# The first stage of a bidirectional encoder layer: from a scheduler's order to one fixed by hand

## The chip, the cores and the metric

The kernel runs on one core of a Trainium2 chip. The metric is device time in microseconds (us) of one execution. The engines named here are PE (TensorE, matrix products), ACT (ScalarE), DVE (VectorE), POOL (GpSimd) and SP (SyncE, which here only issues transfers). Each takes its own instructions strictly in order and waits on semaphores that other engines raise.

## The reference, cut to what matters

One layer runs over 256 tokens of width 2048: a Mamba-2 mixer in both directions, cross-attention into 256 memory tokens, and a gated feed-forward block, each with a norm ahead of it. Only the beginning matters here:

```
u = rmsnorm(h, mix_norm)                    # h = x, 256 x 2048
proj = u @ w_in                             # split into z, xbc (xs, B, C), dt
xbc = silu(dwconv(xbc, conv_w, conv_b))     # centred convolution over positions
dt = softplus(dt_raw + dt_bias)             # 128 columns: 64 heads, two directions
...
y = y_f + y_b + xs * d_skip                 # two chunked scans over (xs, dt, B, C)
y = rmsnorm(y * silu(z), norm_g)
h = h + y @ w_out
```

All inputs are float32, and the result is close to a float32 one.

## The kernel before

Every float32 matrix factor is split in two: `hi`, the value rounded to the type that PE multiplies fast (`F32R`), and `lo`, what is left. A product of two factors is three matmuls: hi x hi, hi x lo and lo x hi (lines 152 to 154 of `gemm_feat`). ACT writes `hi`, and DVE then computes `lo` from the same source and `hi`, so `lo` always comes after `hi`. For a block of weights (128 x 1024, 0.5 MB, `raw`) these are the lines 106 and 107 of `split_plain`; for x they are the lines 101 and 102 of `split_scaled`, one call for each 128 x 256 half of a PSUM bank, with the norm's gain as a scale.

The first stage (lines 242 to 282) works like this. x lies in DRAM with the tokens in rows, so PE turns it (line 260): each quarter of 512 columns takes 8 transposes into two PSUM banks, which ACT and DVE split into the tiles `unit`. DVE also copies each bank to `x_stage` (line 264), and a transfer keeps it in DRAM for the residual sum much later (line 265). ACT squares x and sums each row (line 270) for the norm's factor; the factor is applied after the products, by way of `r_mix`: a sum, a square root (line 220, with a load of the ACT table), some small DVE instructions, two products that spread it over all partitions (line 281) and a copy (line 282). The first products are those of dt: 128 columns, 16 steps of the contraction, 48 matmuls. Then follow the 512 columns of the first block of x (`project(0)`): eight blocks of weights, 24 matmuls each, 192 in all. Then come B and C of the same group, and so on through the layer. PSUM has two tiles for such products (`ps_g`); dt takes one, the first block of x the other, and the one of B and C has to wait until DVE has read dt's bank, which needs `r_mix` (line 297).

No order is written out: a scheduler with a simulated timeline places every instruction on each engine's queue, and so mixes transposes, splits, squares, copies and products. Pools limit how far loads run ahead: five blocks of raw weights, four of split ones.

## Time and profile before

| | before |
|---|---|
| device time, median of 3 runs | 1862.79 us (1862.3 to 1864.23) |
| the profiled execution | 1863.24 us, span 1861.5 us from the first to the last instruction |
| PE busy | 1842.3 us, 99% of the span |
| DVE busy | 1264.2 us, 68% |
| ACT busy | 1018.2 us, 55% |
| DMA | 358.94 MB, mean 193 GB/s |
| granted clock of TensorE, mean | 0.998 |

The span is the profiled execution from its first instruction to its last; the remaining 1.74 us lie around it. Busy time of PE counts a matmul from its start to its modelled end, and matmuls overlap, so a full PE is not one at its peak. The granted clock is a share of 2.4 GHz, so 0.5 stands for 1.2 GHz.

### The profile page before, as it was taken

What the parts mean: (1) busy time and instruction counts of PE and PEld (TensorE: products, weight loads), DVE (VectorE), ACT (ScalarE), POOL (GpSimd) and SP (SyncE); (2) the same over time, 40 slices, a digit from 0 to 9 for tenths busy, and PEclk for the clock granted to TensorE, in tenths of its full rate; (3) what the DMA queues carried; (4) which work ended last, traced back from release to release, by engine and by line L of the source; (5) the groups of instructions that cost most, each with busy time, mean ns of one, the idle gap of its engine ahead of it and who ended that gap; (6) DMA issues with size and microseconds to landing.
All of it is one profiled execution on the core that took longest, in us unless ns stands there. A gap on an engine that the chain in (4) does not pass through costs nothing.

```text
span 1861.5 us, 29854 instructions
## 1 busy us (share of the span) xinstructions
PE 1842.3 (99%) x11821; PEld 1663.5 (89%) x11821; DVE 1264.2 (68%) x1792; ACT 1018.2 (55%) x1454; POOL 2.3 (0%) x11
## 2 busy tenths in 40 slices
PE   8999999999999999999999999999999999999997
PEld 8999999999999988888888888888888888888886
DVE  6878888988887756655555667666664456666654
ACT  6667667766775645444444455555553345555443
POOL 0000000000000000000000000000000000000000
PEclk9999999999999999999999999999999999999999
DMA  8667666766766765655655556566666666666563
GB/s 289 198 203 214 199 189 201 219 197 201 215 182 205 244 197 182 184 177 170 176 176 181 164 187 206 179 189 188 191 191 192 193 192 188 185 187 187 190 193 114
DMA packets 289708, 358.94 MB, mean 193 GB/s; under 512 B 11616, under 2 KB 210656, under 8 KB 289056
## 3 DMA queue, kind: packets, MB, share of 16 engines
q1 hardware_dynamic: 289488, 356.76, 62.3%
q8 instruction: 92, 1.51, 0.3%
q14 instruction: 48, 0.39, 0.1%
q0 software_dynamic: 80, 0.28, 0.1%
HBM read 352.60 MB, written 4.39 MB: 192 GB/s over the span
## 4 chain that ended last, share of the span: by engine, by line
PE 99%; DMA 0%; DVE 0%; ACT 0%; SPq 0%; issue 0%; DVEq 0%
PE psg L169 30%; PE psg L171 16%; PE psg L154 10%; PE psg L153 10%; PE psg L152 10%; PE psm L194 6%; PE psm L193 6%; PE psm L195 6%; PE psm L453 1%; PE psm L448 1%; PE psm L419 1%; PE psm L589 0%; PE psm L591 0%; PE psm L590 0%; DMA x<-in_x_dram 0%; PE psm L405 0%
## 5 line engine op out<-in xcount | busy, mean ns | idle before, releaser
L107 DVE TENSOR_TENSOR w_lo<-raw,w_hi 128x1024 fp32r<-128x1024 f32 x618 | 753.7, 1223 | 499.3 <-ACT w_hi L106 497.1
L106 ACT CAST w_hi<-raw 128x1024 fp32r<-128x1024 f32 x618 | 645.7, 1049 | 684.0 <-PE psg L169 314.5
L169 PE MATMUL psg<-unit,w_hi 128*128 128x512 f32 x2432 | 853.3, 396 | 0.0
L171 PE MATMUL psg<-unit,w_lo 128*128 128x256 f32 x2432 | 683.4, 281 | 0.0
L169 PEld LDWEIGHTS psg<-unit,w_hi 128*128 128x128 f32 x2432 | 456.3, 188 | 106.0
L171 PEld LDWEIGHTS psg<-unit,w_lo 128*128 128x128 f32 x2432 | 460.7, 189 | 0.2
L154 PE MATMUL psg<-unit,w_lo 128*128 128x256 f32 x1552 | 444.8, 287 | 0.1
L152 PE MATMUL psg<-unit,w_hi 128*128 128x256 f32 x1552 | 442.4, 285 | 0.0
L153 PE MATMUL psg<-unit,w_hi 128*128 128x256 f32 x1552 | 441.6, 285 | 0.0
L154 PEld LDWEIGHTS psg<-unit,w_lo 128*128 128x128 f32 x1552 | 298.6, 192 | 3.4 <-issue 3.1
L152 PEld LDWEIGHTS psg<-unit,w_hi 128*128 128x128 f32 x1552 | 298.7, 193 | 1.7 <-issue 1.7
L153 PEld LDWEIGHTS psg<-unit,w_hi 128*128 128x128 f32 x1552 | 298.7, 193 | 0.3 <-issue 0.2
L195 PE MATMUL psm<-w_hi,unit 128*128 128x512 f32 x480 | 187.0, 390 | 0.0
L194 PE MATMUL psm<-w_lo,unit 128*128 128x512 f32 x480 | 187.0, 390 | 0.0
L193 PE MATMUL psm<-w_hi,unit 128*128 128x512 f32 x480 | 186.9, 389 | 0.0
L193 PEld LDWEIGHTS psm<-w_hi,unit 128*128 128x128 f32 x480 | 90.1, 188 | 18.9
L195 PEld LDWEIGHTS psm<-w_hi,unit 128*128 128x128 f32 x480 | 90.1, 188 | 18.8
L194 PEld LDWEIGHTS psm<-w_lo,unit 128*128 128x128 f32 x480 | 90.1, 188 | 18.4
L435 ACT ACTIVATE r<-r,ncum_tok 128x128 f32<-128x128 f32 x128 | 39.4, 390 | 57.5 <-DMA r<-cum_d 57.5
L436 DVE SCALAR_TENSOR_TENSOR r<-r,ncum_tok 128x128 f32<-128x128 f32 x128 | 37.0, 347 | 16.7 <-ACT r L435 16.7
L441 ACT ACTIVATE t<-cb,dt_tok 128x128 f32<-128x128 f32 x128 | 39.1, 389 | 0.7 <-DVE cb L428 0.2
L442 DVE SCALAR_TENSOR_TENSOR t<-cb,dt_tok,t 128x128 f32<-128x128 f32 x128 | 36.5, 349 | 3.3 <-ACT t L441 3.3
(222 smaller groups left out, 1076.4 us busy)
## 6 DMA issues: line engine op xcount, KB each, us to landing
raw<-in_w_up_dram SPq DMA_DIRECT2D x176, 512.0 KB, 3.7
raw<-in_w_in_dram SPq DMA_DIRECT2D x130, 512.0 KB, 4.6
raw<-in_w_down_dram SPq DMA_DIRECT2D x88, 512.0 KB, 3.8
raw<-in_w_out_dram SPq DMA_DIRECT2D x64, 512.0 KB, 4.2
raw<-in_wkv_dram SPq DMA_DIRECT2D x64, 512.0 KB, 3.8
raw<-in_w_in_dram SPq DMA_DIRECT2D x64, 256.0 KB, 4.4
r<-cum_d SPq DMA_DIRECT2D x16, 1024.0 KB, 6.3
raw<-in_wq_dram SPq DMA_DIRECT2D x32, 512.0 KB, 3.5
```

The source lines that it names most:

```text
L106: nc.scalar.copy(out=hi, in_=src)
L107: nc.vector.tensor_tensor(out=lo, in0=src, in1=hi.bitcast(F32), op=ALU.subtract)
L152: nc.tensor.matmul(dst, wh, uh, start=first, stop=False, skip_group_check=True)
L153: nc.tensor.matmul(dst, wh, ul, start=False, stop=False, skip_group_check=True)
L154: nc.tensor.matmul(dst, wl, uh, start=False, stop=last, skip_group_check=True)
L169: nc.tensor.matmul(ps[:, ft, :], hi[:, kk, fs], unit[2][:, kt % 4].rearrange("p s t -> p (s t)"), start=(kt == 0), stop=False, skip_group_ ...
L171: nc.tensor.matmul(ps[:, ft, :T], lo[:, kk, fs], unit[0][:, kt % 4, :], start=False, stop=(kt == nk - 1), skip_group_check=True)
L193: nc.tensor.matmul(banks[tt], uh, hi[:, kk, :], start=(kt == 0), stop=False)
L194: nc.tensor.matmul(banks[tt], uh, lo[:, kk, :], start=False, stop=False)
L195: nc.tensor.matmul(banks[tt], ul, hi[:, kk, :], start=False, stop=(kt == nk - 1))
L435: nc.scalar.activation(out=t1[:, h, :], in_=t1[:, h, :], func=AF.Identity, bias=ncum_tok[:, c, hf:hf + 1])
L441: nc.scalar.activation(out=t2[:, h, :], in_=cb[:, 1, :], func=AF.Copy, scale=dt_tok[:, c, hb:hb + 1])
```

## The change

The first stage is written out in order. `tc.manual_schedule` fixes the order on PE, ACT, DVE and SP for the instructions between its two calls, and the scheduler places only what follows. The steps are small functions: `load_x`, `load_dt`, `load_xw` issue transfers; `busy(n)` issues n products of a tile of ones with itself into an unused bank; `transpose_x`, `split_x`, `keep_x` and `square_x` treat one quarter of x; `split_w` splits a block of weights; `dt_part` and `x_part` issue products. Both PSUM tiles are taken at the start, and the products of the first block of x move from `project(0)` into this stage. The computed values are the same. Ten products of ones are new; no other instruction is added or left out.

```diff
+    def split_raw(raw):
+        hi = sb(ring, [P, raw.shape[1], raw.shape[2]], "w_hi", F32R)
+        lo = sb(ring, [P, raw.shape[1], raw.shape[2]], "w_lo", F32R)
         split_plain(hi, lo, raw)
         return hi, lo
 
+    def load_weights(wv, k0, cols):
+        return split_raw(load_raw(wv, k0, cols))
...
     units_mix = [new_unit() for _ in range(4)]
+    ps_dt, ps_x = psum_g(), psum_g()
     with tc.tile_pool(name="xin", bufs=1) as xin:
+        ordered = tc.manual_schedule(engines={mybir.EngineType.PE, mybir.EngineType.Activation,
+                                              mybir.EngineType.DVE, mybir.EngineType.SP})
+        ordered.__enter__()
         xt = [sb(xin, [P, D], f"x{tt}") for tt in range(2)]
-        dt_w = []
-        for q4 in range(4):
-            if q4 == 2:
-                dt_w.append(load_raw(w_in_v, 0, [(10240, P)]))
+        ss = sb(xin, [P, 2, 4], "x_ss")
+        raws = {}
+        def load_x(u):
             for tt in range(2):
-                nc.sync.dma_start(out=xt[tt][:, q4 * 512:(q4 + 1) * 512],
-                                    in_=x[tt * P:(tt + 1) * P, q4 * 512:(q4 + 1) * 512])
-        ss = sb(xin, [P, 2, 4], "x_ss")
-        for u in range(4):
-            stage = sb(xin, [P, 4, T], "x_stage", bufs=2)
+                nc.sync.dma_start(out=xt[tt][:, u * 512:(u + 1) * 512], in_=x[tt * P:(tt + 1) * P, u * 512:(u + 1) * 512])
+        def load_dt(i):
+            raws["dt", i] = load_raw(w_in_v, 8 * i, [(10240, P)])
+        def load_xw(i):
+            raws["x", i] = load_raw(w_in_v, 2 * i, [(INNER, 512)])
+        def busy(n):
+            for _ in range(n):
+                nc.tensor.matmul(ps_dt[:, 1, :P], ones, ones, start=True, stop=True, skip_group_check=True)
+        def transpose_x(u):
+            out = []
             for jj in range(2):
                 ps = psum_m()
-                for j in range(2):
-                    kt = u * 4 + jj * 2 + j
-                    for tt in range(2):
+                for tt in range(2):
+                    for j in range(2):
+                        kt = u * 4 + jj * 2 + j
                         nc.tensor.transpose(out=ps[:, j * T + tt * P:j * T + (tt + 1) * P],
                                             in_=xt[tt][:, kt * P:(kt + 1) * P], identity=ident)
+                out.append(ps)
+            return out
+        def split_x(u, banks):
+            for jj, ps in enumerate(banks):
                 for j in range(2):
                     split_scaled(units_mix[u], jj * 2 + j, two(ps)[:, j, :], pcol("g_mix", u * 4 + jj * 2 + j))
+        def keep_x(u, banks):
+            stage = sb(xin, [P, 4, T], "x_stage", bufs=2)
+            for jj, ps in enumerate(banks):
                 nc.vector.tensor_copy(out=stage[:, jj * 2:jj * 2 + 2, :], in_=two(ps))
             nc.sync.dma_start(out=xT_d[:, u * 4:(u + 1) * 4, :], in_=stage)
-        dt_bank = gemm_feat(units_mix, w_in_v, [(10240, P)], first_raw=dt_w[0])[0]
-        for q4 in range(4):
+        def square_x(u):
             for tt in range(2):
                 junk = sb(xin, [P, 512], "x_junk")
-                nc.scalar.activation(out=junk, in_=xt[tt][:, q4 * 512:(q4 + 1) * 512], func=AF.Square,
-                                     accum_out=ss[:, tt, q4:q4 + 1])
+                nc.scalar.activation(out=junk, in_=xt[tt][:, u * 512:(u + 1) * 512], func=AF.Square,
+                                     accum_out=ss[:, tt, u:u + 1])
+        def dt_part(i, k0, k1):
+            hi, lo = raws["dt", i]
+            for kt in range(k0, k1):
+                feat_products([ps_dt[:, 0, :]], units_mix, hi[:, kt - 8 * i:kt - 8 * i + 1, :], lo[:, kt - 8 * i:kt - 8 * i + 1, :], kt, 16)
+        def x_part(i):
+            hi, lo = raws["x", i]
+            feat_products([ps_x[:, 0, :], ps_x[:, 1, :]], units_mix, hi, lo, 2 * i, 16)
+        def split_w(kind, i):
+            raws[kind, i] = split_raw(raws[kind, i])
+        load_x(0)
+        load_dt(0)
+        load_xw(0)
+        load_x(1)
+        load_xw(1)
+        busy(6)
+        t = transpose_x(0)
+        split_x(0, t)
+        busy(4)
+        split_w("dt", 0)
+        keep_x(0, t)
+        load_x(2)
+        load_xw(2)
+        dt_part(0, 0, 4)
+        t = transpose_x(1)
+        split_w("x", 0)
+        x_part(0)
+        split_x(1, t)
+        split_w("x", 1)
+        x_part(1)
+        dt_part(0, 4, 8)
+        keep_x(1, t)
+        load_x(3)
+        load_dt(1)
+        load_xw(3)
+        t = transpose_x(2)
+        split_x(2, t)
+        split_w("x", 2)
+        x_part(2)
+        keep_x(2, t)
+        load_xw(4)
+        split_w("x", 3)
+        t = transpose_x(3)
+        x_part(3)
+        split_x(3, t)
+        load_xw(5)
+        split_w("dt", 1)
+        dt_part(1, 8, 12)
+        split_w("x", 4)
+        x_part(4)
+        keep_x(3, t)
+        load_xw(6)
+        square_x(0)
+        square_x(1)
+        dt_part(1, 12, 16)
+        split_w("x", 5)
+        x_part(5)
+        load_xw(7)
+        square_x(2)
+        square_x(3)
+        split_w("x", 6)
+        x_part(6)
+        split_w("x", 7)
+        x_part(7)
+        ordered.__exit__(None, None, None)
+        dt_bank = ps_dt[:, 0, :]
...
         def project(g):
             xs = sb(ssd, [P, 4, T], "xs", bufs=2)
-            conv_silu(gemm_feat(units_mix, w_in_v, [(INNER + g * 512, 512)]), [g * 4 + j for j in range(4)], xs)
+            banks = [ps_x[:, 0, :], ps_x[:, 1, :]] if g == 0 else gemm_feat(units_mix, w_in_v, [(INNER + g * 512, 512)])
+            conv_silu(banks, [g * 4 + j for j in range(4)], xs)
```

On PE, the third quarter of x (banks psm_158 and psm_168) before: its transposes lie among the first products of dt.

```order
L260 MATMUL psm_158<-ident_77,x0_100 128x128 [waits DMAHW5_49,DVE_49,PE_49]
L260 MATMUL psm_158<-ident_77,x1_101 128x128 [waits DMAHW6_49]
L260 MATMUL psm_158<-ident_77,x0_100 128x128
L260 MATMUL psm_158<-ident_77,x1_101 128x128
L152 MATMUL psg_201<-unit_93,w_hi_202 128x256 [waits Activation_49]
L153 MATMUL psg_201<-unit_93,w_hi_202 128x256
L260 MATMUL psm_168<-ident_77,x0_100 128x128 [waits DVE_49,PE_49]
```

On PE, the third quarter now (banks psm_265 and psm_270; w_hi_283 and w_lo_284 are the third block of weights of x, psg_98 its sums).

```order
L146 MATMUL psg_97<-unit_94,w_lo_146 128x256
L277 MATMUL psm_265<-ident_77,x0_104 128x128 [waits DMAHW0_49,PE_49]
L277 MATMUL psm_265<-ident_77,x0_104 128x128
L277 MATMUL psm_265<-ident_77,x1_105 128x128 [waits DMAHW1_49]
L277 MATMUL psm_265<-ident_77,x1_105 128x128
L277 MATMUL psm_270<-ident_77,x0_104 128x128 [waits PE_49]
L277 MATMUL psm_270<-ident_77,x0_104 128x128
L277 MATMUL psm_270<-ident_77,x1_105 128x128 x2
L144 MATMUL psg_98<-unit_94,w_hi_283 128x256 [waits Activation_49]
L145 MATMUL psg_98<-unit_94,w_hi_283 128x256
L146 MATMUL psg_98<-unit_94,w_lo_284 128x256 [waits DVE_49]
```

The eight transposes now stand together, after the last products that the first half of dt's weights allows, and the next instructions behind them are products with the third block of weights.

On ACT before, the same quarter (psm_158, psm_168): squares of x, splits of other banks and casts of weights stand between the halves of one bank.

```order
L101 ACTIVATE unit_95<-psm_158,par_75 128x256 [waits PE_49]
L270 ACTIVATE x_junk_270,x_ss_112<-x1_101 128x512 [waits DMAHW6_49,Activation_49]
L101 ACTIVATE unit_94<-psm_146,par_75 128x256 [waits DVE_49]
L101 ACTIVATE unit_95<-psm_168,par_75 128x256 [waits PE_49]
L270 ACTIVATE x_junk_272,x_ss_112<-x0_100 128x512 [waits DMAHW7_49,Activation_49]
L106 CAST w_hi_232<-raw_230 128x1024 [waits DMAHW1_49]
L101 ACTIVATE unit_95<-psm_158,par_75 128x256 [waits DVE_49]
L270 ACTIVATE x_junk_274,x_ss_112<-x1_101 128x512 [waits DMAHW0_49,Activation_49]
L106 CAST w_hi_362<-raw_360 128x1024 [waits DMAHW2_49]
L101 ACTIVATE unit_95<-psm_168,par_75 128x256 [waits DVE_49]
```

On ACT now, the same quarter (psm_265, psm_270), from the cast before it to the two behind it.

```order
L106 CAST w_hi_215<-raw_115 128x1024 [waits DMAHW6_49]
L101 ACTIVATE unit_95<-psm_265,par_75 128x256 [waits PE_49]
L101 ACTIVATE unit_95<-psm_265,par_75 128x256 [waits DVE_49]
L101 ACTIVATE unit_95<-psm_270,par_75 128x256 [waits PE_49]
L101 ACTIVATE unit_95<-psm_270,par_75 128x256 [waits DVE_49]
L106 CAST w_hi_283<-raw_155 128x1024 [waits DMAHW2_49]
L106 CAST w_hi_317<-raw_263 128x1024 [waits DMAHW7_49,Activation_49]
```

The four halves of a quarter now follow each other directly, and the cast of the weights stands behind them. The wait on DVE in each second half is for DVE's `lo` of the first half of the same bank.

On SP now, the third and the fourth store of turned x (x_stage) and the loads of weights behind them.

```order
L291 DMA xT_d_90<-x_stage_311 128x1024 [waits DMAHW0_49,DVE_49]
L115 DMA raw_315<-in_w_in_dram 128x2x512 [waits DMAHW1_49,Activation_49]
L115 DMA raw_363<-in_w_in_dram 128x2x512 [waits DMAHW2_49,Activation_49]
L291 DMA xT_d_90<-x_stage_409 128x1024 [waits DMAHW3_49,DVE_49]
L115 DMA raw_413<-in_w_in_dram 128x2x512 [waits DMAHW4_49,Activation_49]
L115 DMA raw_463<-in_w_in_dram 128x2x512 [waits DMAHW7_49,DMAHW5_49,Activation_49]
```

Before, all of x, both blocks for dt and the first three blocks for x were issued ahead of the first store; now two or three loads stand behind each store, and each store waits for two DVE copies.

## Rows read from the trace of the kernel before

**Rows 1.** The page, part 4: shares of the chain that ended last, by engine.

```profile
PE 99%; DMA 0%; DVE 0%; ACT 0%; SPq 0%; issue 0%; DVEq 0%
```

**Rows 2.** Windows: stretch (us), its length, busy us (x instructions) per engine, PEclk, DMA share, GB/s.

```profile
12.00:60.00 48.00, 48.00 (x386) 48.00 (x386) 41.60 (x74) 32.76 (x49) 0.00 (x0) 1.00 0.81 259
60.00:540.00 480.00, 479.90 (x4027) 468.65 (x4026) 397.44 (x725) 327.24 (x559) 0.00 (x0) 1.00 0.68 203
600.00:1800.00 1200.00, 1200.00 (x6688) 1045.18 (x6687) 742.24 (x856) 588.40 (x728) 0.00 (x0) 1.00 0.61 188
```

**Rows 3.** Timeline of PE, first stage: start, us busy, what [idle before <- releaser].

```profile
5.16 1.54 PE L260 MATMUL psm<-ident,x 128*128 128x128 f32 x6 [0.73 <-DMA x<-in_x_dram]
...
11.82 0.56 PE L152 MATMUL psg<-unit,w_hi 128*128 128x256 f32 x1
...
12.40 1.05 PE L260 MATMUL psm<-ident,x 128*128 128x128 f32 x4
13.10 0.56 PE L154 MATMUL psg<-unit,w_lo 128*128 128x256 f32 x1
13.46 0.41 PE L152 MATMUL psg<-unit,w_hi 128*128 128x256 f32 x1
...
16.45 0.40 PE L154 MATMUL psg<-unit,w_lo 128*128 128x256 f32 x1
16.66 0.31 PE L152 MATMUL psg<-unit,w_hi 128*128 128x256 f32 x1
```

**Rows 4.** Timeline of PE around the two products of r_b.

```profile
31.82 0.61 PE L281 MATMUL psm<-ident,r_b 128*128 128x128 f32 x4
32.18 0.36 PE L154 MATMUL psg<-unit,w_lo 128*128 128x256 f32 x1
32.38 0.28 PE L152 MATMUL psg<-unit,w_hi 128*128 128x256 f32 x1
32.50 0.28 PE L153 MATMUL psg<-unit,w_hi 128*128 128x256 f32 x1
```

**Rows 5.** Timeline of ACT in the first stage.

```profile
6.36 0.20 ACT L318 ACTIVATE a_neg<-par 128x1 f32<-128x1 f32 x1 [0.43 <-DMA par<-in_params_dram]
6.47 0.46 ACT L101 ACTIVATE unit<-psm,par 128x256 fp32r<-128x256 f32 x1
...
7.82 0.82 ACT L101 ACTIVATE unit<-psm,par 128x256 fp32r<-128x256 f32 x2
8.53 0.63 ACT L270 ACTIVATE x_junk<-x 128x512 f32<-128x512 f32 x1
...
9.14 0.83 ACT L101 ACTIVATE unit<-psm,par 128x256 fp32r<-128x256 f32 x2
9.92 1.05 ACT L106 CAST w_hi<-raw 128x1024 fp32r<-128x1024 f32 x1
...
18.82 1.28 ACT L220 ACT_TABLE_LOAD   x1
```

**Rows 6.** Timeline of DVE in the first stage.

```profile
6.96 0.48 DVE L102 SCALAR_TENSOR_TENSOR unit<-psm,par,unit 128x256 fp32r<-128x256 f32 x1 [0.21 <-ACT unit L101]
...
21.11 1.28 DVE L264 COPY x_stage<-psm 128x512 f32<-128x512 f32 x2
22.31 1.22 DVE L107 TENSOR_TENSOR w_lo<-raw,w_hi 128x1024 fp32r<-128x1024 f32 x1
...
32.98 0.42 DVE L282 COPY r_mix<-psm 128x256 f32<-128x256 f32 x1
33.43 0.42 DVE L297 TENSOR_TENSOR r<-psg,r_mix 128x256 f32<-128x256 f32 x1
```

**Rows 7.** Transfers into raw in the first 30 us, by tile.

```profile
DMA to landing us min/median/max: 4.4/7.0/8.7
```

**Rows 8.** Windows at the end of the span, columns as in rows 2.

```profile
1850.00:1851.00 1.00, 0.39 (x2) 0.00 (x0) 0.57 (x1) 0.52 (x2) 0.00 (x0) 1.00 0.00 0
...
1853.00:1854.00 1.00, 0.00 (x0) 0.00 (x0) 1.00 (x5) 0.72 (x1) 0.00 (x0) 0.54 0.00 0
```

More of the change, by code (lines that the diff above doesn't have):

```diff
@@ L117, in load_raw @@
         return raw
-    def load_weights(wv, k0, cols, raw=None):
-        width = sum(n for _, n in cols)
-        kc = 1024 // width
-        if raw is None:
-            raw = load_raw(wv, k0, cols)
-        hi = sb(ring, [P, kc, width], "w_hi", F32R)
-        lo = sb(ring, [P, kc, width], "w_lo", F32R)
+    def split_raw(raw):
+        hi = sb(ring, [P, raw.shape[1], raw.shape[2]], "w_hi", F32R)
+        lo = sb(ring, [P, raw.shape[1], raw.shape[2]], "w_lo", F32R)
         split_plain(hi, lo, raw)
@@ L127, in load_weights, with feat_products @@
         return hi, lo
+    def load_weights(wv, k0, cols):
+        return split_raw(load_raw(wv, k0, cols))
     def kview(w):
         return w.rearrange("(kt p) n -> p kt n", p=P)
-    def gemm_feat(units, wv, cols, k_first=0, first_raw=None):
+    def feat_products(banks, units, hi, lo, k0, nk):
+        nft = hi.shape[2] // P
+        for kk in range(min(hi.shape[1], nk - k0)):
+            kt = k0 + kk
+            uh = units[kt // 4][0][:, kt % 4, :]
+            ul = units[kt // 4][1][:, kt % 4, :]
+            for ft in range(nft):
+                dst = banks[ft // 2][:, (ft % 2) * T:(ft % 2 + 1) * T]
+                wh = hi[:, kk, ft * P:(ft + 1) * P]
+                wl = lo[:, kk, ft * P:(ft + 1) * P]
+                first = kt == 0 and ft % 2 == 0
+                last = kt == nk - 1 and (ft % 2 == 1 or ft == nft - 1)
+                nc.tensor.matmul(dst, wh, uh, start=first, stop=False, skip_group_check=True)
+                nc.tensor.matmul(dst, wh, ul, start=False, stop=False, skip_group_check=True)
+                nc.tensor.matmul(dst, wl, uh, start=False, stop=last, skip_group_check=True)
@@ L134, in gemm_feat @@
+    def gemm_feat(units, wv, cols):
         width = sum(n for _, n in cols)
-        nft = width // P
-        kc = 1024 // width
         nk = 4 * len(units)
         ps = psum_g()
-        banks = [ps[:, b, :] for b in range((nft + 1) // 2)]
-        for k0 in range(0, nk, kc):
-            hi, lo = load_weights(wv, k_first + k0, cols, first_raw if k0 == 0 else None)
-            for kk in range(kc):
-                kt = k0 + kk
-                uh = units[kt // 4][0][:, kt % 4, :]
-                ul = units[kt // 4][1][:, kt % 4, :]
-                for ft in range(nft):
-                    dst = banks[ft // 2][:, (ft % 2) * T:(ft % 2 + 1) * T]
-                    wh = hi[:, kk, ft * P:(ft + 1) * P]
-                    wl = lo[:, kk, ft * P:(ft + 1) * P]
-                    first = kt == 0 and ft % 2 == 0
-                    last = kt == nk - 1 and (ft % 2 == 1 or ft == nft - 1)
-                    nc.tensor.matmul(dst, wh, uh, start=first, stop=False, skip_group_check=True)
-                    nc.tensor.matmul(dst, wh, ul, start=False, stop=False, skip_group_check=True)
-                    nc.tensor.matmul(dst, wl, uh, start=False, stop=last, skip_group_check=True)
@@ L155, in gemm_feat @@
+        banks = [ps[:, b, :] for b in range((width // P + 1) // 2)]
+        for k0 in range(0, nk, 1024 // width):
+            hi, lo = load_weights(wv, k0, cols)
+            feat_products(banks, units, hi, lo, k0, nk)
         return banks
```

## The prediction

> **What bounds the kernel now.** I read the chain of waits first: it is PE to 99% [rows 1], so what counts is when PE gets its work, and nothing else. The table by stretches says where it lacks it: from 12 us on PE is full in each stretch, with 0.1 us missing between 60 and 540 us and nothing between 600 and 1800 [rows 2]. So a delay of the first stage is paid in full at the end, and a gain there is kept in full. The timeline of PE then shows the first stage. Before 11.82 us there are only transposes, which wait for x. The first product starts at 11.82 and the third, the first one with a `lo` of weights, at 13.10; behind that no wait is left. From 13.46 to 16.45 a product follows every 0.21 us (14 steps in 2.99 us), which is 1.2 GHz, and 0.12 us from there on, which is 2.4 GHz [rows 3, 4]. Four transposes take 0.70 us at the lower clock (12.40 to 13.10), so I count 0.35 at the higher.
>
> The measure for the new order is the start of the products of B and C, since the work ahead of it on PE is the same in both kernels but for the ten products of ones: 32 transposes, 240 products, two for `r_b`. In the old order 103 products stand between `r_b` and that point, so it lies at 32.18 + 103 x 0.12 = 44.5 us [rows 4].
>
> **The price of one quarter of x.** Now a quarter's four halves stand in a row on ACT and DVE, with the cast of the next weights behind them. A half costs ACT 0.46 and DVE 0.48, and DVE begins 0.03 after ACT ends (6.47 + 0.46 = 6.93, then 6.96) [rows 5, 6]. The second half of a bank waits for DVE's first, so it starts at 0.46 + 0.03 + 0.48 + 0.03 = 1.00; the third, in the other bank, follows it after 0.36 (two in 0.82 us [rows 5]); DVE reaches that one at 1.89, after its own second; the fourth waits for it until 2.40. The cast starts at 2.8 and takes 1.05: `hi` is there at 3.85, and `lo`, 1.22 us later, at 5.1 [rows 5, 6]. The Trainium skill agrees that this wait has to be there: "PSUM — Partial Sum Buffer", section "PSUM bank collisions raise a hardware error", says that ScalarE and VectorE must not read one bank at the same time. In the old order the wait exists too, but other work fills it (6.47, then a square, then halves of other banks).
>
> **The walk.** First quarter: ACT's first half comes at 6.47 as before, since `a_neg` ahead of it waits for the parameters until 6.36 [rows 5]. The first product follows at 10.35 and the third at 11.6, both 1.5 us earlier than before. The ten products of ones hide in waits: two full-clock ones take 0.36 us [rows 4], so six at the lower clock take 2.2 and end at 4.6, ahead of the second half of x at 5.16 [rows 3]; four more end at 8.0, ahead of 10.35. If that cover were gone they would cost 3.6 us.
> From 11.6 ten products at 0.21 reach 13.7 and eight transposes 15.1. The first block of x (24 products) waits for nothing: its `lo` comes at 14.05 behind two copies (1.28 us) [rows 6]. I let the clock rise at 16.5, where it did in the old order [rows 3]; then the block ends at 18.6.
> Second quarter: ACT starts at 14.7, since its four transposes end at 14.4, so the second block's `hi` is there at 18.6 and its `lo` at 19.85. PE does two products and waits 1.0 us. 22 products and the 12 of dt end at 23.95, the third quarter's transposes at 24.65.
> Third quarter: nothing lies behind these transposes on PE but the block whose cast is behind this quarter on ACT. ACT starts at 24.6, so PE waits until 28.5 (3.8 us), does two products, and waits 1.0 us for `lo`, until 29.75.
> Fourth quarter: 22 products, 8 transposes and 24 products with weights that are ready end at 36.0. The second block of dt is cast behind the quarter, at 35.85: PE waits 0.95 and 1.0 us, and goes on at 38.2. The next three pieces (10 + 24 + 12 + 24 products) have their weights in time and end at 46.6.
> Seventh block: eight squares (0.61 us each, 8.53 to 9.14) and a table load of 1.28 [rows 5] put its cast at 45.25 and its `lo` at 47.5: 0.7 us of waiting.
> End: x ends at 53.45 with the two products of `r_b`, the second of which is now PE's last instruction before B and C. Copy and multiplication, each 0.42 us, free the PSUM tile (32.98 to 33.85 [rows 6]): 1.1 us of waiting, until 54.6.
> So the point moves from 44.5 to 54.6: 10.1 us later. Of these 9.5 are the waits listed (1.0 + 3.8 + 1.0 + 0.95 + 1.0 + 0.7 + 1.1).
>
> **Two terms that the trace of before bounds only.** Transfers: now loads stand on SP behind the store of a quarter, which waits for its copies. The fifth block's load goes out at 31.5 and is needed at 36.85; the seventh's goes out at 41.0 and is needed at 45.25. Landing took 4.4 us at least, 7.0 in the median and 8.7 at most [rows 7]. At 4.4 the first is in time and the second 0.15 late; at 7.0 they are 1.65 and 2.75 late, which adds to 4.4 us. The median was taken with a dozen transfers under way at once; here three are, so I go by the lower end, at 5.1 us, and count 0.7. Loading ahead of the need could not gain anything, since the waits named are not for transfers.
> Clock: at the end of the span PE does its last work at 1850.39, and the row of 1853 to 1854 has it at 0.54, which is nearly all at 1.2 GHz [rows 8]. My wait of 3.8 us, with two products and another 1.0 behind it, is about as long as that pause. If the clock falls, the 22 products from 29.75 on take 0.093 us more each, 2.05 us, and the eight transposes behind them 0.7 in all if it has not risen by then. So the bounds are 0 and some 2.7 us, and I take 2.1, since the row at the end is the nearest. The Trainium skill speaks against the change here: "TensorE: Matmul & The Clock Gate", section "HAM oscillation — how this bites in real kernels", says that bursts of products with pauses between them lose the clock in each pause. By it the sum has the 2.1 us, without it not.
>
> **Sum.** 10.1 + 0.7 + 2.1 = 12.9 us. The profiled execution took 1863.24 us (span 1861.5 and 1.74 around it), so 1876.1; the median of the runs is 0.45 below that execution, so 1875.7 us.
>
> **Rivals.**
> 1. The waits come, and the clock stays up: 1875.7 - 2.1 = 1873.6. For it speaks that the two waits of the third quarter are cut by two products.
> 2. Transfers land as late as the median before: 4.4 in place of 0.7, so 1879.4. For it: each load must wait for a store; against it: far less is under way.
> 3. The halves of a quarter do not alternate with DVE, because the semaphore has been raised already. Then a quarter costs 1.3 us less, and this counts at the first, third and fourth: 10.1 - 3.9 = 6.2, with late transfers 6.9, and no long pause for the clock: 1869.7. Against it: in the table of the order the second half waits for the DVE instruction directly behind the first.
> 4. Faster: the head start decides. PE begins its run at 11.6 in place of 13.1 (-1.5), and the ten products of ones lift the clock before it, so that the 18 products at 0.21 and eight transposes run at the full clock (-1.7, -0.7). That gives 1862.79 - 3.9 = 1858.9. It decides if PE's waits behind 11.6 us add to less than 3.9 us; I count 9.5. It needs ACT and DVE to keep ahead of PE, and the third quarter alone gives them 4.8 us of serial work with PE empty.
>
> **How the numbers follow.** Chances: the forecast 0.45, rival 1 0.30, rival 2 0.11, rival 3 0.07, rival 4 0.04, and 0.03 for a mixture that ends near zero. About 0.2%, 3.7 us, is what a measurement of this kernel can tell from no change. All but the last two cases are slower by more than that: slower 0.93, same 0.03, faster 0.04. The range of 8 in 10 runs from rival 3, 1869.5, to a little above rival 2, 1881.
>
> **What would show it.** In the new trace: first product near 10.4; PE waiting for ACT some 3.8 us behind the third quarter's transposes and then 1.0 for DVE; shorter pairs of that kind at the second block, at the second half of dt and at the seventh block; 1.1 us ahead of B and C; products at 0.21 us behind the long wait if the clock falls. B and C start near 57.4. Wrong would be a PE without waits behind 12 us, a wait for a transfer among the longest, or a later stage whose waits change, since I count everything behind the first stage as merely moved.

## The result, and the profile after

The changed kernel takes 1880.04 us (median of 6 runs, 1878.25 to 1881.27) against 1863.18 us (1862.30 to 1866.95, 6 runs) for the kernel before on the same chip: ratio 1.0088, 95% interval 1.0078 to 1.0099. It is slower by some 16.9 us. Its profiled execution took 1881.27 us with a span of 1879.5 us.

In the table by stretches (columns as in [rows 2]) PE lacks 9.1 us between 12 and 60 us, where it lacked nothing before, and the granted clock there is 0.86. Up to 74 us some 1.1 us more are missing; from there to 540 us, and from 600 on, PE is full again.

```profile
12.00:60.00 48.00, 38.88 (x261) 37.11 (x262) 26.77 (x42) 23.75 (x42) 0.00 (x0) 0.86 0.67 206
...
74.00:540.00 466.00, 466.00 (x3905) 455.21 (x3905) 388.54 (x702) 316.72 (x537) 0.00 (x0) 1.00 0.68 202
...
600.00:1800.00 1200.00, 1200.00 (x6754) 1047.58 (x6754) 748.45 (x865) 590.24 (x731) 0.00 (x0) 1.00 0.61 189
```

The waits of PE in the first 75 us, by line and by what it waited for (us in total, times, longest): two engines, ACT and DVE, make nearly all of them from the first product on (11.45 us).

```profile
PE psg L144 <- ACT w_hi L106: 8.1, 5, 3.5
PE psg L146 <- DVE w_lo L107: 3.7, 5, 0.8
PE psg L268 <- POOL ones L84: 2.4, 1, 2.4
PE psm L277 <- DMA x<-in_x_dram: 1.3, 1, 1.3
PE psg L144 <- DVE r L392: 1.1, 1, 1.1
```

The timeline of PE answers to [rows 3, 4]: L277 are transposes, L268 the products of ones, L144 to L146 the three products.

```profile
7.06 0.88 PE L277 MATMUL psm<-ident,x 128*128 128x128 f32 x6 [1.33 <-DMA x<-in_x_dram]
7.78 1.06 PE L268 MATMUL psg<-ones 128*128 128x128 f32 x8
11.45 0.38 PE L144 MATMUL psg<-unit,w_hi 128*128 128x256 f32 x1 [2.61 <-ACT w_hi L106]
...
12.70 0.39 PE L146 MATMUL psg<-unit,w_lo 128*128 128x256 f32 x1 [0.76 <-DVE w_lo L107]
...
25.25 1.03 PE L277 MATMUL psm<-ident,x 128*128 128x128 f32 x8
29.79 0.39 PE L144 MATMUL psg<-unit,w_hi 128*128 128x256 f32 x1 [3.50 <-ACT w_hi L106]
...
31.05 0.58 PE L146 MATMUL psg<-unit,w_lo 128*128 128x256 f32 x1 [0.65 <-DVE w_lo L107]
31.42 0.41 PE L144 MATMUL psg<-unit,w_hi 128*128 128x256 f32 x1
...
35.90 1.51 PE L277 MATMUL psm<-ident,x 128*128 128x128 f32 x8
...
51.84 0.39 PE L144 MATMUL psg<-unit,w_hi 128*128 128x256 f32 x1 [1.04 <-ACT w_hi L106]
53.10 0.39 PE L146 MATMUL psg<-unit,w_lo 128*128 128x256 f32 x1 [0.76 <-DVE w_lo L107]
...
60.42 0.38 PE L376 MATMUL psm<-ident,r_b 128*128 128x128 f32 x2
61.87 0.36 PE L144 MATMUL psg<-unit,w_hi 128*128 128x256 f32 x1 [1.07 <-DVE r L392]
...
592.27 0.39 PE L146 MATMUL psg<-unit,w_lo 128*128 128x256 f32 x1 [0.76 <-DVE w_lo L107]
```

The row at 61.87 is the start of B and C. Before, the same product (the 240 of dt and of the first block of x stand ahead of it) starts at 44.62; the prediction had reckoned 44.5.

```profile
44.62 0.28 PE L152 MATMUL psg<-unit,w_hi 128*128 128x256 f32 x1
```

So B and C start 17.3 us later, and the profiled executions differ by 18.0 (1881.27 and 1863.24). The delay of the first stage is paid in full; the other 0.8 is the wait at 592.27, which the kernel before does not have. The profiled execution of the changed kernel is the slowest of its six, 1.2 us above their median.

How a quarter costs so much is seen on ACT in the third one (answers to [rows 5]): its four halves (L101) alternate with DVE, and the cast (L106), for which PE waits, stands behind all four.

```profile
25.89 0.47 ACT L101 ACTIVATE unit<-psm,par 128x256 fp32r<-128x256 f32 x1 [6.13 <-PE psm L277]
26.91 0.84 ACT L101 ACTIVATE unit<-psm,par 128x256 fp32r<-128x256 f32 x2 [0.55 <-DVE unit L102]
28.33 0.47 ACT L101 ACTIVATE unit<-psm,par 128x256 fp32r<-128x256 f32 x1 [0.58 <-DVE unit L102]
28.70 1.03 ACT L106 CAST w_hi<-raw 128x1024 fp32r<-128x1024 f32 x1
```

From the first half to the cast it is 2.81 us; the prediction had 2.8. ACT itself stood idle for 6.13 us ahead of it, waiting for PE's transposes: PE and ACT wait for each other in turn.

The granted clock (the column after the five engines) falls three times. Each fall stands behind waits: 2.61 and 0.76 at 11.45 to 12.70, 3.50 and 0.65 at 29.79 to 31.05, and 1.04 and 0.76 at 51.84 to 53.10.

```profile
12.00:13.00 1.00, 0.30 (x2) 0.30 (x3) 1.00 (x2) 0.34 (x1) 0.00 (x0) 0.98 0.02 8
13.00:16.00 3.00, 3.00 (x16) 3.00 (x15) 1.98 (x3) 0.10 (x1) 0.00 (x0) 0.50 0.46 169
...
31.00:35.00 4.00, 3.95 (x18) 3.96 (x19) 2.42 (x3) 1.04 (x1) 0.00 (x0) 0.50 0.49 144
35.00:37.00 2.00, 2.00 (x12) 2.00 (x11) 0.00 (x0) 0.00 (x1) 0.00 (x0) 0.53 0.94 312
...
50.00:54.00 4.00, 2.21 (x16) 1.80 (x16) 3.00 (x9) 2.15 (x4) 0.00 (x0) 0.99 1.13 318
54.00:56.00 2.00, 2.00 (x11) 2.00 (x11) 1.52 (x2) 1.24 (x2) 0.00 (x0) 0.50 1.17 290
```

### The profile page after: what moved, and what is told of

It reads as the page before. It is cut to its first block, busy times and chain, and to the rows that moved or that the text cites. A ratio compares the mean times of both kernels' runs of the same rounds, so it can differ in the third digit from the quotient of the medians.

```text
span 1879.5 us, 29886 instructions
## 1 busy us (share of the span) xinstructions
PE 1849.3 (98%) x11841; PEld 1669.2 (89%) x11841; DVE 1266.1 (67%) x1792; ACT 1019.8 (54%) x1454; POOL 2.3 (0%) x11
## 4 chain that ended last, share of the span: by engine, by line
PE 97%; DVE 1%; ACT 1%; DMA 1%; issue 0%; SPq 0%; DVEq 0%; ACTq 0%
PE psg L171 30%; PE psg L173 15%; PE psg L146 10%; PE psg L144 10%; PE psg L145 10%; PE psm L197 6%; PE psm L195 6%; PE psm L196 6%; PE psm L549 1%; PE psm L544 1%; PE psm L515 1%; PE psm L687 0%; PE psm L685 0%; PE psm L686 0%; PE psm L501 0%; DVE w_lo L107 0%
## 5 line engine op out<-in xcount | busy, mean ns | idle before, releaser
L106 ACT CAST w_hi<-raw 128x1024 fp32r<-128x1024 f32 x618 | 645.8, 1049 | 684.1 <-PE psg L171 315.8
L144 PE MATMUL psg<-unit,w_hi 128*128 128x256 f32 x1552 | 443.9, 286 | 9.2 <-ACT w_hi L106 8.1
L146 PE MATMUL psg<-unit,w_lo 128*128 128x256 f32 x1552 | 445.9, 287 | 4.4 <-DVE w_lo L107 4.4
L144 PEld LDWEIGHTS psg<-unit,w_hi 128*128 128x128 f32 x1552 | 299.6, 193 | 12.1 <-ACT w_hi L106 10.4
L146 PEld LDWEIGHTS psg<-unit,w_lo 128*128 128x128 f32 x1552 | 299.6, 193 | 9.0 <-DVE w_lo L107 5.8
```

Source lines behind the costliest of these rows:

```text
L106: nc.scalar.copy(out=hi, in_=src)
L144: nc.tensor.matmul(dst, wh, uh, start=first, stop=False, skip_group_check=True)
L146: nc.tensor.matmul(dst, wl, uh, start=False, stop=last, skip_group_check=True)
```

## The experiments

The theory: PE waits for casts that stand on ACT and DVE behind whole quarters of x, the waits cost the clock as well, and both are paid at the end. The rivals: something else in the change (the products of ones, the early PSUM tiles, the split of the loops) costs the time; or the loads that stand behind stores do. Every edit below is to the changed kernel. "B and C" is the start of their products in the profiled execution. The runs were spread over several chips, and each ratio is to the kernel before on the chip of that run.

| run | median us | ratio to before (95%) | profiled us | B and C |
|---|---|---|---|---|
| before | 1863.18 | | 1863.24 | 44.62 |
| changed | 1880.04 | 1.0078 to 1.0099 | 1881.27 | 61.87 |
| no fixed order | 1863.72 | 0.9993 to 1.0012 | 1867.37 | 46.67 |
| ones in the third wait | 1875.56 | 1.0052 to 1.0082 | 1877.13 | 57.23 |
| casts first | 1877.46 | 1.0062 to 1.0092 | 1879.03 | 58.19 |
| banks in turn | 1875.06 | 1.0049 to 1.0079 | 1872.63 | 54.99 |
| casts and loads first | 1877.09 | 1.0062 to 1.0092 | 1878.42 | 55.46 |
| no ones | 1879.99 | 1.0078 to 1.0108 | 1879.84 | 60.08 |
| all three, six ones | 1872.01 | 1.0039 to 1.0069 | 1871.89 | 51.26 |
| tuned order | 1867.21 | 1.0015 to 1.0036 | 1866.40 | 46.41 |
| tuned, r inside | 1863.32 | 0.9991 to 1.0009 | 1862.64 | 43.40 |
| more ones at first | 1880.07 | 1.0078 to 1.0105 | 1878.12 | 58.72 |
| ones at the seventh block | 1878.67 | 1.0067 to 1.0098 | 1878.64 | 59.66 |
| ones in all three | 1874.93 | 1.0047 to 1.0074 | 1873.38 | 55.01 |

Profiled time less B and C lies between 1817.6 and 1820.8 us in all rows but one (casts and loads first, 1823.0): to some 3 us all the kernels have the same rest, and the first stage parts them. One profiled execution is one draw: in banks in turn it is 2.4 us below the median, in no fixed order 3.7 above.

**No fixed order.** The two lines that switch the scheduler off are gone; the rest of the change stays.

```
-        ordered = tc.manual_schedule(engines={...})
-        ordered.__enter__()
...
-        ordered.__exit__(None, None, None)
```

> The changed kernel with its two calls of the manual schedule taken out, so that the scheduler orders the first stage too; ones products, early PSUM tiles and the moved products stay. Theory (the order written by hand makes PE wait): the waits behind 12 us go, B and C start near 45 to 46 us, and the time is back at the old one, 1863 to 1866 us. Rival (the ten products of ones, the PSUM tiles taken early or the products cut into pieces cost the time): it stays above 1872 us.

It is level with the kernel before. Its profiled execution is the slowest of ten, and in it x landed late (PE waits 3.03 us for x until 10.95), so B and C start at 46.67 and not at 45 to 46 as expected. Behind 12 us PE has one wait, the 1.07 ahead of B and C:

```profile
45.00 0.60 PE L372 MATMUL psm<-ident,r_b 128*128 128x128 f32 x4
46.67 0.36 PE L144 MATMUL psg<-unit,w_hi 128*128 128x256 f32 x1 [1.07 <-DVE r L388]
```

So nothing else in the change costs time that can be measured: the order does.

**Ones in the third wait.** 18 products of ones stand between the third quarter's transposes and the third block.

```
         t = transpose_x(2)
         split_x(2, t)
+        busy(18)
         split_w("x", 2)
```

> Eighteen products of ones are added behind the third quarter's transposes, where PE waits 3.5 us for ACT; they take 18 x 0.18 = 3.2 us and fill the wait without filling it up. Theory (the pause lets the clock fall, and the fall costs 2.8 us: 22 products and 8 transposes at the lower rate from 31 to 37 us): those run at 0.12 us, B and C start 2.8 us earlier, near 59, and the time is 1877 us. Rival (the slow products have another cause, such as waits on operands): the time stays at 1880 us or rises by what the added products cost.

The products behind the wait now follow at 0.12 us:

```profile
25.50 4.18 PE L268 MATMUL psg<-ones 128*128 128x128 f32 x36
...
30.43 0.39 PE L146 MATMUL psg<-unit,w_lo 128*128 128x256 f32 x1 [0.50 <-DVE w_lo L107]
30.65 0.28 PE L144 MATMUL psg<-unit,w_hi 128*128 128x256 f32 x1
30.77 0.28 PE L145 MATMUL psg<-unit,w_hi 128*128 128x256 f32 x1
...
33.16 1.03 PE L277 MATMUL psm<-ident,x 128*128 128x128 f32 x8
```

From that `lo` product to the fourth quarter's transposes it takes 2.73 us (33.16 less 30.43), in the changed kernel 4.85 (35.90 less 31.05). B and C come 4.6 earlier, more than the 2.8 expected. Of these the clock there gives 2.6 (2.1, and 0.5 from the eight transposes, which take 0.79 in place of 1.27). Ahead of it 0.6 is won, since x landed earlier in this execution (first product at 10.63; third block's first `lo` product at 30.43 in place of 31.05). At the seventh block 0.8 is won, since its cast does not wait for its weights here (PE waits 0.23 us for it in place of 1.04). The last 0.6 is what arrives of the fall at the seventh block, which does not come (granted clock 1.00 from 47 to 57 us). So 2.6 is what the filled wait shows; filled with useless products, this wait costs less than left empty.

**Casts first.** The casts of the third block and of the second half of dt's weights go ahead of the halves of x.

```
         t = transpose_x(2)
-        split_x(2, t)
         split_w("x", 2)
+        split_x(2, t)
...
+        split_w("dt", 1)
         split_x(3, t)
         load_xw(5)
-        split_w("dt", 1)
```

> The casts of the third block of weights and of the second block of dt's weights go ahead of the splits of the third and fourth quarter on ACT and DVE. Theory (each wait hides the next one): PE no longer waits behind the third quarter's transposes, but the fourth block of weights lands only near 31.5 us, since its load stands behind a store that waits for DVE's copies, so PE waits some 3 us there instead; 0.5 to 2 us are gained, 1878 to 1879.5 us. Rival (the order of cast and split alone makes the wait): 3.5 + 0.65 us of waiting and 2.8 us of lower clock go, 1873 us.

The third block runs on without a wait, and the same wait comes at the fourth block: 33.70 with 3.66 us for ACT, whose cast waited for its weights until 32.60, and the clock falls behind it (granted clock 0.59 from 34 to 38 us).

```profile
33.70 0.39 PE L144 MATMUL psg<-unit,w_hi 128*128 128x256 f32 x1 [3.66 <-ACT w_hi L106]
```

Only 2.6 us of the median are won, a little more than expected (0.5 to 2), with executions from 1875.27 to 1879.88. **Casts and loads first** then puts each load ahead of the store that it stood behind:

```
+        load_x(3)
+        load_dt(1)
+        store_x(0)
...
         split_w("x", 2)
+        split_x(2, t)
```

> As the order with the casts ahead of the third and fourth quarters' halves, but every load of weights and of x also goes out on SP ahead of the store that it stood behind. There the wait of PE for ACT had only moved to the fourth block (3.66 us at 33.70), whose weights landed late. If the late loads are what held that cast, this wait is under 1 us, the products of B and C start 3 to 5 us earlier than there (58.19), at 53 to 55, and the time is 1872 to 1874. If not the loads but ACT's own queue of halves holds it, a wait of 3 us or more stays, B and C start at 57 to 59, and the time is 1876 to 1878.

The wait at the fourth block is down to 1.41 us, for `lo`, and none is left for the cast, so the late loads had held that cast, and B and C start at 55.46, half a microsecond later than expected. The time did not follow at all: 1877.09, a miss by 3 us. Now the chain to r is late, and a last fall of the clock takes more:

```profile
52.70 0.68 PE L384 MATMUL psm<-ident,r_b 128*128 128x128 f32 x4 [2.88 <-DVE r_b L383]
55.46 0.55 PE L144 MATMUL psg<-unit,w_hi 128*128 128x256 f32 x1 [2.07 <-DVE r L400]
```

PE then works at a granted clock of 0.50 from 55 to 61 us: 26 matmuls in 5.54 us, where the full clock needs some 3.1 (26 x 0.12). That 2.4 lies behind the start of B and C, and brings this kernel's 1823.0 near the rest of the table. A shorter fall at this place is in three other rows too: ones in the third wait (0.59 from 57 to 61 us), casts first (0.58 from 58 to 62) and the tuned order (0.59 from 46 to 50).

**Banks in turn.** Each quarter's halves go through its two banks in turn, so that ACT has the next half while DVE works on the last.

```
-            for jj, ps in enumerate(banks):
-                for j in range(2):
+            for j in range(2):
+                for jj, ps in enumerate(banks):
```

> The four halves of a quarter are split in turns of the two banks (first halves of both, then second halves). Theory (a second half waits for DVE on the first half of its bank): a quarter's chain on ACT falls from 2.8 to about 1.8 us, the first product comes 1 us earlier (10.4), the long wait falls from 3.5 to about 2.5 us, and 3 us are gained over the first, third and fourth quarter, 1877 us; if the shorter pause keeps the clock up, 2.8 us more, 1874 us. Rival (the halves do not wait for each other's bank): no change, 1880 us.

ACT now does the four halves of the third quarter in one piece, and the cast starts 1.83 us after the first (25.40 less 23.57), not 2.81:

```profile
23.57 1.94 ACT L101 ACTIVATE unit<-psm,par 128x256 fp32r<-128x256 f32 x4 [6.13 <-PE psm L277]
25.40 1.03 ACT L106 CAST w_hi<-raw 128x1024 fp32r<-128x1024 f32 x1
```

The long wait is 2.52 in place of 3.50, and B and C come at 54.99. So the alternation on one bank is real, and it costs 1.0 us a quarter; it is one part of the waits and not the whole. The median, 1875.06, lies between the two values expected, but the four executions reach from 1872.63 to 1878.07, and the trace is that of the fastest. The 6.9 us by which B and C come earlier there are more than the alternation: x landed earlier, and the clock is 1.00 at the seventh block (46 to 55 us).

**No ones.** `busy(6)` and `busy(4)` are left out.

> The hand order without the ten products of ones in the first quarter. If they lie in waits, as the forecast had it, the first product starts where it did (10.4 to 11.5) and the time stays within 2 us of 1880: at most the products and transposes at the lower clock ahead of 16.6 go on a little longer, up to +1.0 us. If the ones themselves hold up the transposes of the first quarter, the first product comes 1 us earlier or more and the time falls to 1878 to 1879.

The median did not move: 1879.99. The first product starts at 11.39, as in the changed kernel (11.45), though x landed a microsecond earlier. So the ten ones cost nothing that can be measured. B and C start at 60.08, 1.8 earlier, since the third fall does not come in this execution (1.00 from 49 to 60 us).

**More ones at first, at the seventh block, in all three.** The one number `busy(4)` ahead of the first product becomes 14; or `busy(4)` is added ahead of the seventh block; or both, with the 18 of above.

```
-        busy(4)
+        busy(14)
         split_w("dt", 0)
...
+        busy(18)
         split_w("x", 2)
...
         split_w("x", 6)
+        busy(4)
         x_part(6)
```

> One number of the changed kernel: 14 products of ones in place of 4 between the first quarter's transposes and the first product. In the changed kernel the clock was full from 7.8 us on, and fell behind the wait of 2.61 us (PEclk 0.98 in 12 to 13, 0.50 in 13 to 16). If the wait is what loses it, ones that fill it keep it: no products at 0.21 between 13 and 16.5, eight transposes in 0.7 in place of 1.5, the second block of x some 1.6 us earlier, and B and C 0.8 to 2 us earlier (a transfer or the copy behind the last lo may take part of it back): 1878 to 1879.5. If the clock is lost whatever PE does there, or the ones hold up the first product, the time stays at 1880 or goes above it.

The first of the three kernels. In the trace it is as expected: from 13 to 16 us the granted clock is 1.00 and 28 matmuls fit, where the changed kernel had 16.

```profile
13.00:16.00 3.00, 3.00 (x28) 3.00 (x27) 2.12 (x4) 1.45 (x4) 0.00 (x0) 1.00 0.75 255
```

B and C start 3.2 us earlier, at 58.72, of which 1.2 are x that landed earlier (first product 10.22). The median, 1880.07, did not follow, and the times leave it open: two executions took 1878.0 and 1878.1, two 1882.0 and 1882.5, and what happened in the latter no trace shows.

> The changed kernel with four products of ones (1.0 us) ahead of the seventh block, in the wait of 1.04 us for its hi. There the clock fell a second time (products at 0.21 from 53.9 to 57.4, PEclk 0.50). If the two waits of about 1 us with two products between them are what loses it, it stays up: PE ends r_b 1.6 us earlier. But DVE then has the last lo ahead of the copy to r_mix, as without the ones (there PE was done at 57.45 and B and C started at 60.08), so B and C come only 0.5 to 1.0 earlier than 61.87, and the time is 1879 to 1879.6, hardly to be told from 1880. If the second fall costs its full 1.6, it is 1878.4 with B and C at 60.3. If it falls all the same, nothing moves.

The third fall is gone (52 to 56 us: 36 matmuls at 1.00), and as expected a good part of it does not arrive: from the seventh block's first `lo` product to B and C it takes 8.02 us (51.64 to 59.66) where it took 8.77 (53.10 to 61.87), 0.75 less and not 1.6. PE is through with `r_b` at 57.85 (57.25 and 0.60), but DVE has another `lo` ahead of the copy, and B and C wait 1.80 us:

```profile
57.50 1.23 DVE L107 TENSOR_TENSOR w_lo<-raw,w_hi 128x1024 fp32r<-128x1024 f32 x1 [0.89 <-ACT w_hi L106]
58.64 0.42 DVE L378 COPY r_mix<-psm 128x256 f32<-128x256 f32 x1
59.09 0.42 DVE L393 TENSOR_TENSOR r<-psg,r_mix 128x256 f32<-128x256 f32 x1
```

> Products of ones in all three waits of the changed kernel at once: 14 in the first quarter, 18 behind the third quarter's transposes, 4 ahead of the seventh block. The order of ACT, DVE and SP stays as it is. This parts the loss into waits and clock. If the clock adds to the waits, no product between 12 us and r_b comes at 0.21, and the 1.6, 2.8 and 1.6 us that the three falls cost in the changed kernel's trace come off on PE; of the last, the copy to r_mix behind the last lo takes about 1 us back (wait ahead of B and C 1.8 to 2.5 in place of 1.1), and a fall behind that wait may take 1.4 us more. So B and C start at 54 to 56 and the time is 1874 to 1876; what is left above the kernel before is waits that only another order can take away. If the clock were most of the loss, B and C would start at 50 or earlier, at 1870 or less. If filling one wait only moves the loss to the next, the time stays at 1877 or more.

This parts the loss. The clock is 1.00 from 12 to 54 us, and B and C (55.01) and the median (1874.93) lie inside what was expected; the wait ahead of B and C is 1.39, less than I had thought, and no fall follows it (1.00 from 54 to 60 us as well):

```profile
12.00:54.00 42.00, 37.98 (x310) 36.56 (x308) 25.72 (x42) 23.32 (x41) 0.00 (x0) 1.00 0.75 225
```

So of the 17.3 us that B and C moved, 10.4 are left without any fall of the clock (55.01 less 44.62): waits, now part filled with ones. The steps from one `lo` product to the next part the other 6.9: 1.0 is x that landed late in the changed kernel's profiled execution (first product 11.45 and here 10.43); 1.3, 2.6 and 1.2 are the three falls, as far as they arrive; and 0.8 is the seventh block, whose cast waited for its weights there (0.70 us of idle ACT) and does not here.

**All three, and the tuned orders.** Banks in turn, casts early and loads ahead of stores together, without the four ones ahead of the first product (the expectation says that the ones are gone, but the six ahead of the transposes stay in this kernel); then the same aims with the transposes of a quarter among the products of the block ahead of it, copies late, and 16 ones ahead of the first product.

```
         busy(6)
         t0 = transpose_x(0)
         split_x(0, t0)
         busy(10)
         split_w("dt", 0)
         t1 = transpose_x(1)
         dt_part(0, 0, 4)
         split_w("x", 0)
         x_part(0)
         split_x(1, t1)
         split_w("x", 1)
         x_part(1)
...
         t2 = transpose_x(2)
         split_w("x", 2)
```

> The hand order with three things changed together: halves of a quarter go through the two banks in turn, every load goes ahead of the stores, each quarter's transposes and the cast of the next weights go ahead of the halves of the quarter behind, and the ones are gone. If the waits of PE for the casts (8.1 for hi, 3.7 for lo) and the clock that falls behind them make the whole loss, hardly a wait is left behind 17 us and B and C start at 47 to 50: 1866 to 1869, 3 to 6 us above the kernel before. If something else of an order fixed by hand costs time (the waits for semaphores at each step, say), waits stay that no cast explains, and the time is 1872 or more. Faster than before (under 1859) is what the earlier first product alone would give.

A miss by 3 us, to the time that the rival gave, but the trace does not show the rival's reason: it has waits for casts of 1.97, 0.75, 0.92 and 0.46 up to 17 us (the first since dt's weights, now loaded behind both of the first two quarters of x, land late: ACT waits 2.17 us for them), behind them the clock stays down until 23 us, and there is one of 2.08 for r ahead of B and C:

```profile
18.00:20.00 2.00, 2.00 (x12) 2.00 (x11) 1.29 (x2) 0.00 (x0) 0.00 (x0) 0.50 0.91 240
20.00:22.00 2.00, 2.00 (x11) 2.00 (x11) 0.00 (x0) 0.00 (x0) 0.00 (x0) 0.50 1.10 401
```

> Another hand order with the same aims: banks in turn, loads ahead of stores, products of ones kept (6 and 10), copies later still, the second and third quarters' transposes among the products of x. If waits for casts and the clock make the whole loss, what is left is a start of the first product at 10 to 11 us and a wait of some 3 to 4 us ahead of B and C, since the copy of r waits for the last copies on DVE: B and C at 47 to 50 and 1866 to 1869. If the clock also stays up (no products at 0.21 behind 17 us) the lower end holds; if the wait ahead of B and C lets it fall, some 1 to 2 us come on top. A rival that a hand order cannot reach the scheduler's says 1870 or more.

1867.21, as expected, with B and C a little earlier than expected. Its PE has two waits of 0.47 and 0.35 for `lo` up to 17 us, none from there to 42.5, and then the wait for r:

```profile
42.51 0.60 PE L384 MATMUL psm<-ident,r_b 128*128 128x128 f32 x4
46.41 0.55 PE L144 MATMUL psg<-unit,w_hi 128*128 128x256 f32 x1 [3.30 <-DVE r L400]
```

The last run takes that wait away: squares earlier on ACT, and the chain to r inside the order.

```
         square_x(3)
         split_w("x", 5)
+        norm_x()
...
+        norm_x2()
...
         x_part(6)
         split_w("x", 7)
+        spread_r()
         x_part(7)
```

> The tuned hand order (banks in turn, loads ahead of stores, 6 and 16 products of ones) with the squares moved earlier on ACT, and with r_x, r_b, the copy to r_mix and the multiplication of dt by it all inside the order, ahead of the last block's products. In the tuned order PE was full from 16.5 us to the end of x at 43.1, and only 3.3 us of waiting for r stood ahead of B and C (46.41), with some 1.0 us of products at the lower clock behind it. If that wait was all that was left, B and C start at 43 to 44 without a wait, and the time is 1861.5 to 1863.5: level with the kernel before or up to 1.5 us ahead. If a hand order has a cost that does not come from waits of PE, it stays at 1865 or more although B and C start at 44 or earlier.

```profile
39.59 0.60 PE L323 MATMUL psm<-ident,r_b 128*128 128x128 f32 x4
43.40 0.36 PE L144 MATMUL psg<-unit,w_hi 128*128 128x256 f32 x1 [0.34 <-DVE xr L325]
```

B and C start 1.2 us earlier than before, the profiled execution is 0.6 us shorter, and the medians are level: 1863.32 and 1863.37, ratio 1.0000 (0.9991 to 1.0009). So an order by hand costs nothing of itself that can be measured, and this one wins nothing that can be measured either.

## Why the prediction was right, point by point

It said 1875.7 us, with a range of 1869.5 to 1881 and slower at 0.93; 1880.04 is inside, 4.3 above. Mechanism and places held; some sizes and one event did not. Rival 2's 1879.4 lies nearer to the measured time than the forecast, but that is chance: its reason is not in the trace, as shown below.

- **What bounds it, and the measure.** Right in the main: B and C 17.3 us later, 18.0 us at the end. By the prediction's own signs two things were off, both small: a wait for a transfer is among the longest (1.33 us for x at 7.06), and a later stage has a new wait (0.76 at 592.27).
- **The price of a quarter.** Right (2.81 and 2.8), and with it the wait behind the third quarter's transposes: 3.50 and 0.65 in place of 3.8 and 1.0. The shorter pairs came where they were put: 0.33 and 0.76 at the second block (1.0 was forecast), 0.63 and 0.76 at the second half of dt (0.95 and 1.0). Rival 3, halves that do not alternate, is out; the run with banks in turn shows what it would have been worth, 1.0 us a quarter.
- **The start of the walk.** It had the first product at 10.35, from the execution before, where ACT began at 6.47. Here the second half of x came at 7.06 in place of 5.16 (answers to [rows 3]), ACT began at 7.54, and all is some 1.3 us later by the third block. This is the execution and not the change: with ones in the third wait, in the same order up to there, no transpose waited for x.
- **Clock at the third quarter.** Taken as 2.1 between bounds of 0 and 2.7; measured 2.6 against the run with ones in the third wait. The upper end was the right one, since the clock was still down through the eight transposes. The Trainium skill's rule on pauses between bursts, which the prediction drew from "TensorE: Matmul & The Clock Gate", section "HAM oscillation — how this bites in real kernels", speaks of this effect, and for the long wait the trace agrees: granted clock 0.50 from 31 to 35 us behind it, and 1.00 there once it is filled. For each pause, as the prediction put it, the trace does not agree: behind 0.33 and 0.76 us at the second block the clock stays at 1.00 (19 to 24 us). Rival 1 is out.
- **Clock in the first quarter.** Right in size, wrong in reason, and so luck: the walk let the clock rise at 16.5 as before. In fact the ones had raised it by 7.1 us (six transposes in 0.88 us, before in 1.54), and the wait of 2.61 lost it again. Rival 4 had this half right, that ones lift the clock, and did not ask whether it would outlast the wait behind them.
- **A third fall, at the seventh block.** Not foreseen: the prediction priced the clock only for the long wait. It stands behind waits of 1.04 and 0.76 us, and PE lost 1.5 us from 53.9 to 57.3 (16 products at 0.093 more each). It does not come in every execution of this order: with ones in the third wait and without ones, where the first of the two waits is 0.23 and 0.22, the clock stays up.
- **Squares.** 0.61 each from [rows 5]; measured 0.76, since the read of the row sum stands behind each square. In the row that was used for the price the next instruction starts beside that read; here the next square starts when it has ended. From the cast of dt's second block until ACT is free for the seventh block's cast it is 10.2 us (39.81 to 50.04) in place of 9.4 (35.85 to 45.25).
- **Transfers.** 0.7 us taken (5.1 us of landing makes 0.85 by the prediction's own times) and 0.70 found, as idle time of ACT ahead of the seventh block's cast at 50.75, 5.85 us after its load went out at 44.90 behind the store. The row names PE as the releaser, but PE had long been past the block in question, so I read it as the transfer. In the run with more ones at first the row of the same cast does name the transfer (0.47 us ahead of 47.60), and with ones in the third wait the cast waits for nothing (46.75). So this term is 0 to 0.7 from one execution to the next, and that it came out at the forecast's number is luck. Rival 2 (4.4 us) is out.
- **The end.** 1.1 us ahead of B and C, measured 1.07.

The rows of ACT on which the squares and the transfer rest:

```profile
41.70 0.63 ACT L296 ACTIVATE x_junk<-x 128x512 f32<-128x512 f32 x1
42.23 0.19 ACT L296 ACTIVATION_READ_ACCUMULATOR x_junk<-x 128x1 f32 x1
42.45 0.64 ACT L296 ACTIVATE x_junk<-x 128x512 f32<-128x512 f32 x1
...
50.75 1.04 ACT L106 CAST w_hi<-raw 128x1024 fp32r<-128x1024 f32 x1 [0.70 <-PE psg L145]
```

From the forecast's 57.4 to 61.87 it is 4.5 us: 1.3 for the start, 0.5 for the clock, 0.9 for the squares and 1.5 for the third fall make 4.2. The start belongs to this execution, which is itself 1.2 us above the median. The term that was off the most is the clock: it was taken at one wait, at 2.1, and measured 2.6 there and 1.5 more at the seventh block.

## What to carry to other kernels

When an order is fixed by hand, write beside each product which engine makes its last operand and what stands ahead of that on its queue; a cast behind a whole quarter of other work is a wait of that length. Ask of each wait, the short pairs too, what follows if the clock falls, and price it for the products behind it, not for the wait alone. A wait that is removed shows the next in line (here casts, then loads, then the chain to r), so judge a step by the start of the next stage together with the clock behind it.

## What the runs showed of the hardware

- Waits of 1.04 and 0.76 us with two products between them took the clock from 1.00 to 0.50 (51.8 to 57.4 us in the changed kernel). At 19.81 and 21.07, with 0.33 and 0.76, it held, and so it did at 40.90 and 42.16, with 0.63 and 0.76. A single wait of 1.5 us at 577 us in the kernel before left it at 1.00 as well. The length of the waits alone does not decide it: 1.00 and 0.75 at the seventh block left it at 1.00 in casts first (48 to 56 us), 0.80 and 0.76 there took it to 0.57 in more ones at first (50 to 54); and ahead of B and C 2.08 us (all three, six ones) and 2.63 (no ones) left it at 1.00, while 1.92 (ones in the third wait) did not. What else decides, no run here shows.
- Where the clock had not been up yet, the column of the granted clock reads 1.00 while products follow at 0.21 us (before, 13 to 16 us, and the run without ones). Only the distance between products tells there.
- How many useless products fill a wait matters: in the first quarter four left 2.61 us empty, and the clock fell behind it; fourteen left 0.37, and it held.
